# Moving the start addresses of on-chip tiles in a one-core attention block, and splitting two weight blocks one stage earlier

## The chip, the cores and the metric

The kernel runs on one core of one Trainium2 chip. The metric is the device time of one execution in microseconds. A core has TensorE (PE, matrix multiplication; its weight loads are listed apart as PEld), VectorE (DVE), ScalarE (ACT), GpSimd (POOL) and SyncE (SP, which issues most of the DMAs). Data lie in SBUF, 128 partitions of some 200 KB each; matmuls write to PSUM, in banks of 512 fp32 columns.

## The reference

One sub-layer of a hybrid encoder, in fp32, on x of 1024 tokens by 1024 channels. Cut to what matters:

```python
h = rms_norm(x, g_pre)
a_qkv, bq, bk, bv, mq, ga, gb, gm, mg = split(h @ w_in)      # 1024 x 10496 weights in all
# A: 24 heads in 3 groups, dilated sliding windows (128,1) (512,4) (2048,16), rope, merged by their lse
# B: 8 query heads on 2 key heads, qk-norm, 2-D axial rope, full attention over 1024 tokens
# M: 4 heads, cross-attention into 256 memory tokens (mem normed, @ w_mem_kv)
ya, yb, ym = (oa * silu(ga)) @ w_br_a, (ob * silu(gb)) @ w_br_b, (om * silu(gm)) @ w_br_m
merged = sum(sigmoid(mg + b_merge)[i] * y[i])                # per channel, 3 branches
return x + rms_norm(merged @ w_out, g_post)
```

## The kernel before

**Arithmetic.** An fp32 product is made of three matmuls on float32r operands: each operand is split into a high part h (an ACT copy that rounds) and a low part l = x - h (a DVE subtraction), and the products h·h, h·l and l·h are added in PSUM. `split` (lines 104 to 106) makes the two parts. The normalised x, transposed, stands in SBUF all the time as hh0 to hh7 and hl0 to hl7, each 128 channels by 1024 tokens.

**Stages, in order.** The key and value projection of B and the start of the gates and of the memory (`kv_proj`, `add_gate`, `add_kv`, lines 363 to 560); the projections of bq and mq with the memory attention woven in (`b_q`, `mq_unit`, `m_att`); B's attention with projection units of the merge gates woven in (`b_att`, `add_filler`, lines 654 to 795); the value stage (lines 799 to 1037), which makes the values of branch A; the pair stage (lines 1038 to 1359), which makes the remaining gates, A's queries and keys and the remaining merge gates; A's attention with the branch outputs woven in (lines 1360 to 1758); the output projection (lines 1759 to 1838).

**The value stage.** `steps_v` is a list of 44 steps. Steps 0 to 15 are a plain product, 8 blocks for each half of the tokens; steps 16 to 43 (FIRST = 16) are the seven products of Strassen's scheme in Winograd's form, 4 blocks each, in the order of `PRODUCTS`. A step issues 12 matmuls (line 983: four banks by three parts), then the evacuation of an earlier product (`left`), the splits and loads that are due two and five steps later, and the sums of weights. POOL makes the sums S1 to S4, ACT and DVE the splits. Steps FIRST + 24 to FIRST + 27 also split the four blocks of T2 (sums of the token operand, loaded from DRAM), which the pair stage needs; T1, T2, T3 and T4 are kept for the whole pair stage. The last evacuations follow the loop (`v_out`, `v_store`): DVE adds, ACT scales and issues the store.

**The pair stage.** `pairs` lists 26 pairs of 128-column weight units; each pair is again seven products of 12 matmuls (`prod`, line 1093, 26 x 7 x 12 = 2184 matmuls). The order of the products over the pairs is written out in `START` and `order`: (0,1), (0,2), (0,4), (0,3), (1,1), (0,5), and so on, where (n, x) is product x of pair n. TensorE works strictly in this order. After the matmuls of a product, the program queues the evacuation of the product before, and then `tasks(n, x)`: which blocks are split (`block_of`), which blocks of T3 are split (`split_block`), which weights are summed on POOL (`weight_sum`) and which are loaded. ACT, DVE, POOL and SP take their work in the order of the program in both stages (a manual schedule from line 801). Pair 0's blocks S1 and S2 lie in a `wh` and a `wl` buffer (two of each), all others in `ch` buffers. Product 4 takes S1 and T1, product 3 S2 and T2, product 5 S3 and T3. `own_blocks(n)` splits A11 and A12 of pair n.

**Where tiles lie.** Tiles are taken from two ends of SBUF, in the order of the program, each pool behind the one before, each tile rounded up to 32 bytes. At the lower end the first 1152 bytes are taken, then follow the constants: cs (1704 bytes, rounded to 1728), ones, mhalf, rb, rcol, nrcol, rsq and hbm, up to byte 7264 of each partition, which is 14 x 512 + 96. There hh0 begins; as hh, hl, wr, wh and wl are 4096 bytes each and nothing small is between, all of them begin at 96 past a multiple of 512. The pools that come and go behind them (start, qn, ba, tb, vp, sr, aa, mg) begin there too, and so do their tiles, until a small tile stands ahead: behind bnm (272 bytes) QH and QL begin at 160, and bp at 256 past a multiple of 512. The upper end is at byte 229,344, which is 447 x 512 + 480; the tiles of kvl, ml, t23, tr, rope and aqk, and with them KS, kmh, T1, T2, T3, aq and ak, begin at 480 past a multiple of 512, and wbh and wbl, behind small tiles, at 416. A streamed operand of 512 fp32 columns is 2048 bytes of a partition, a block of weights of 128 columns 512 bytes, so a slice of a tile has the remainder of its tile.

Of the kernel before, what the change touches and what calls it, by code (L numbers as in the profile page):

```python
# [8 lines left out]
F32 = mybir.dt.float32  # L9
R = mybir.dt.float32r  # L10
# [5 lines left out]
S = 1024  # L16
NT = 8
P = 128
# [32 lines left out]
def block(ctx: ExitStack, tc: tile.TileContext, x, xT, memT, cst, msk, bcst, tabA, gpost,  # L51
# [4 lines left out]
    const = ctx.enter_context(tc.tile_pool(name="const", bufs=1))  # L56
# [32 lines left out]

    cs = const.tile([P, C_END], F32, name="cs")  # L90
    nc.sync.dma_start(cs, cst)
    ident = cs[:, C_ID:C_ID + 128]
    ones = const.tile([P, 1], F32, name="ones")
    V.memset(ones, 1.0)
# [9 lines left out]
    def split(dst_h, dst_l, src):  # L104
        A.activation(dst_h, src, AF.Copy)  # L105
        V.tensor_tensor(dst_l, src, dst_h.bitcast(F32), op=OP.subtract)  # L106
# [130 lines left out]
    def pool(name, side="left"):  # L237
        p = tc.tile_pool(name=name, bufs=1, side=side, reuse_waits="tile")
        return p, p.__enter__()

    def close(p):
        p.__exit__(None, None, None)

    startp, st = pool("start")
    kvp, kvl = pool("kvl", "right")
    mlp, ml = pool("ml", "right")
# [199 lines left out]
    for k in range(8):  # L446
        if k % 2 == 0:
            load_wkv(k // 2)
        for e in range(2 if k == 0 else 1):
            t = slice(e * 512, e * 512 + 512) if k == 0 else slice(0, S)  # L450
# [29 lines left out]
    for c in range(2):  # L480
        t = st.tile([P, 4, 256], F32, name=f"mt{c}", tag=f"xk{c}")
# [327 lines left out]
    T1, T2, T3 = [], [], []  # L809
# [5 lines left out]
    def wslot(j):  # L815
        return wp.tile([P, 1024], R, name=("wh", "wl")[j])
# [40 lines left out]
    def parts_of(t):  # L857
        return t[:, lo], t[:, hi]
# [98 lines left out]
    def weight_sum(n, j, to):  # L957
        u, v, op = {1: lambda: (part(n, 2), part(n, 3), OP.add), 2: lambda: (to[1], part(n, 0), OP.subtract),
                    3: lambda: (part(n, 0), part(n, 2), OP.subtract),
                    4: lambda: (part(n, 1), to[2], OP.subtract)}[j]()  # L960
        G.tensor_tensor(to[j], u, v, op=op)
# [10 lines left out]
    for n, (i, e, k) in enumerate(steps_v):  # L972
        if k == 0:
            now = v_banks()
        for j in range(4):
            if i is None:
                t = slice(e * 512 + j * 128, e * 512 + j * 128 + 128)
                (bh, bl), w, end = (hh[k][:, t], hl[k][:, t]), v_first[k], 7
            else:
                (bh, bl), w, end = tokens_at(i, k, j), SB[i, k], 3  # L980
            wh_, wl_ = parts_of(w)
            for q, (a, b) in enumerate(((bh, wh_), (bl, wh_), (bh, wl_))):
                PE.matmul(now[j], a, b, start=k == 0 and q == 0, stop=k == end and q == 2)
        behind = left.pop(0)() if left else []
        if n + 2 < 8 and n + 2 >= 4:
            v_first.append(slots0[n - 2])
            split(*parts_of(v_first[-1]), raw1[:, n - 2])
        if 6 <= n < 20 and n % 4 == 2:
            x_scale(n // 4 - 1)
        m = n + 2 - FIRST  # L990
        if 0 <= m < 28:
            split_at(*divmod(m, 4))
        for f in behind:
            f()
        m = n + 5 - FIRST
        if 0 <= m < 28:
            blocks_at(*divmod(m, 4))
        for nm, s0 in (("S1", 7), ("S3", 11), ("S2", 17), ("S4", 21)):
            if 0 <= n - s0 < 4:
                sum_at(nm, n - s0)  # L1000
        if 6 <= n < 20 and n % 4 == 3:
            x_blocks(n // 4 - 1)
            if n < 19:
                x_load(n // 4)
        if n == 4:
            nc.sync.dma_start(rl, lbd.rearrange("h (a b) -> (h a) b", b=64))
        if n == 8:
            V.reciprocal(rl, rl)
            nc.sync.dma_start(rld.rearrange("h (a b) -> (h a) b", b=64), rl)
        if 0 <= n - FIRST - 24 < 4:  # L1010
            h, l = parts_of(T2[n - FIRST - 24])
            split(h, l, l.bitcast(F32))
        if n == FIRST + 10:
            for j in range(2):
                nc.sync.dma_start(tab[j], tabA[:, j])
        if n == FIRST + 17:
            V.tensor_tensor(tab[0], tab[0], rb, op=OP.mult)
            G.tensor_tensor(tab[1], tab[1], rb, op=OP.mult)
        if n == FIRST + 16:
            load_pair(0, 0)  # L1020
            load_pair(0, 1)
        if n == FIRST + 21:
            own_blocks(0)
        if n - FIRST in (15, 16):
            t_load("T2", T2, n - FIRST - 15)
        if n - FIRST in (19, 23):
            t_load("T3", T3, (n - FIRST - 19) // 4)
        if k == end:
            for j in range(4):
                if i is None:  # L1030
                    left.append(lambda b=now[j], T=4 * e + j: [lambda: v_store(rs(), VG[0], T, b)])
                else:
                    left.append(lambda i=i, j=j, b=now[j]: v_evac(i, j, b))
# [26 lines left out]

    def block_of(n, nm):
        src = part(n, 3) if nm == "A22" else SF[int(nm[1])]
        if n == 0 and nm in ("S1", "S2"):
            h, l = parts_of(wslot(int(nm[1]) - 1))
        else:
            t = CH.pop() if CH else sr.tile([P, 2, 512], R, name="ch", bufs=5)
            h, l = t[:, 0], t[:, 1]
        split(h, l, src)
        BL[n][nm] = h, l

# [141 lines left out]

    def tasks(n, x):
        if n < 2:
            blocks = {(0, "1"): [(0, "S1"), (0, "S2")], (0, "4"): [(0, "S3")], (1, "1"): [(1, "S1")], (0, "5"): [(0, "A22")],
                      (1, "4"): [(0, "S4")], (0, "7"): [(1, "S2")], (0, "6"): [(1, "S3")], (1, "3"): [(1, "A22")],
                      (1, "2"): [(1, "S4")], (1, "5"): [(2, "S1")], (1, "7"): [(2, "S3")], (1, "6"): [(2, "A22")]}.get((n, x), ())
        else:
            blocks = {"1": [(n, "S2")], "2" if n < last else "3": [(n, "S4")]}.get(x, [])
            if n < last:  # L1220
                blocks = {"7": [(n + 1, "S3")], "6": [(n + 1, "A22")], "5": [(n + 1, "S1")]}.get(x, blocks)
        for m, nm in blocks:
            block_of(m, nm)
        for nm, k in {(0, "1"): [("T3", 0), ("T3", 1)], (0, "2"): [("T3", 2)],
                      (0, "4"): [("T3", 3)]}.get((n, x), ()):
            split_block(nm, k)
        j = {(0, "2"): 1, (0, "4"): 2, (0, "3"): 3, (1, "4"): 4}.get((n, x))
        if j:
            weight_sum(1, j, SF)
        if n == 0:  # L1230
            if x == "5":
                for u in range(2):
                    load_pair(2, u)
        elif n < last:
            if x == "3":
                own_blocks(n + 1)
            j = {"4": 1, "3": 2, "2": 3, "5": 4}.get(x) if n > 1 else {"3": 1, "2": 2, "5": 3}.get(x)
            if j:
                weight_sum(n + 1, j, SF)
            if n == 1 and x == "5":  # L1240
                weight_sum(2, 4, SF)
            if x == ("4" if n > 1 else "3") and n + 2 <= last:
                load_pair(n + 2, 0)
                load_pair(n + 2, 1)
        if x in "325":
            for u, y in ((1, "3"), (0, "2")):
                if x == y:
                    rope_add(n - 1, u)
            for u, y in ((1, "2"), (0, "5")):
                if x == y:  # L1250
                    rope_store(n - 1, u)
        if n == last - 1 and x in "46" or n == last and x == "1":
            if x != "6":
                m_load(wp.tile([P, S], F32, name="wr", bufs=WR))
            if x != "1":
                m_load(sr.tile([P, S], F32, name="rw", bufs=2))
        if n == last and x in "4352":
            for k in (0, 1) if x in "45" else (2, 3):
                t = lo if x in "43" else hi
                split(hh[k][:, t], hl[k][:, t], MB[k][:, t])  # L1260
# [105 lines left out]
    with tc.tile_pool(name="aa", bufs=1, reuse_waits="tile") as aa:  # L1366
# [190 lines left out]
        def combine(p_):  # L1557
# [2 lines left out]
            c, wgt = {}, [None] * 3  # L1560

            def fetch():
                c["t"] = cb.tile([32, 3, 2, 64], F32, name="cpt", bufs=1)
                nc.sync.dma_start(c["t"].rearrange("c g q i -> c g (q i)"),
                                  std[p_].rearrange("g (c x) -> c g x", c=32))

# [94 lines left out]
        LR = []  # L1661

        def lse_load():
            LR.append(cb.tile([16, 512], F32, name="lse"))
            for b in range(2):
                nc.sync.dma_start(LR[0].rearrange("r (h b i) -> b r h i", h=4, b=2)[b],
                                  std[3, 0:2].rearrange("g (t b h i) -> b (g t) h i", t=8, b=2, h=4)[b])
# [295 lines left out]
```

## Time and profile before

| what | value |
| --- | --- |
| time before, median of 3 runs | 1427.84 us (1427.16 to 1429.21) |
| the profiled execution | 1427.6 us, span 1425.8 us |
| TensorE busy | 1401.5 us, 7547 instructions |
| DVE, ACT, POOL busy | 947.3, 657.9, 543.9 us |
| DMA | 204.26 MB, mean 143 GB/s |
| TensorE's mean granted clock | 0.998 |

The profile is one execution, taken by the hardware. A line such as "L1093 PE MATMUL s<-T,ch" names the code line, the engine, the operation, the tile written and the tiles read, the streamed operand first and the weights second, buffer numbers left out. Float32r is shown as f32. In the timeline, the first column is the start of an instruction in microseconds from the start of the span and the second its duration; consecutive equal instructions stand in one row with their count. Matmuls are pipelined: each takes about 0.39 us from start to end, and the next starts long before that end, so the rate is read from the starts. In brackets stands the idle time of the engine before an instruction, and what ended it. "PEclk" is the share of full clock that TensorE was granted.

### The profile page before, as it was taken

The page shows a single profiled execution, that of the slowest core. Times are in us where ns is not written, and L with a number is a line of the kernel's source. Part 1 is how long each engine was busy: PE and PEld are TensorE (multiplying, and loading weights), DVE is VectorE, ACT ScalarE, POOL GpSimd, SP SyncE. Part 2 cuts the span into 40 slices and gives each one's busy share as a digit, 9 for nine tenths or more (in the row PEclk, how much of TensorE's full clock was granted, in tenths as well). Part 3 has the DMA queues.
Part 4 walks back from the last instruction along what each step waited for, and adds up shares of the span by engine and source line. Part 5 has one row for each costly group of instructions (what it writes and reads, how often), then busy time and mean ns, then how long its engine had stood idle before and what let it go on. Part 6 is the DMA issues. An engine that isn't in the chain of part 4 may idle for free.

```text
span 1425.8 us, 21181 instructions
## 1 busy us (share of the span) xinstructions
PE 1401.5 (98%) x7547; PEld 1119.0 (78%) x7547; DVE 947.3 (66%) x1703; ACT 657.9 (46%) x1434; POOL 543.9 (38%) x437
## 2 busy tenths in 40 slices
PE   7999999999999999999999999999999999999998
PEld 7899986666657887888888888888877777777887
DVE  7765468677652477977777877655766666867543
ACT  6553355666653454443222232344447766732221
POOL 0415604677674312322554455433300012346322
PEclk9999999999999999999999999999999999999999
DMA  6342011011007674332655565756568578736223
GB/s 234 110 120 75 16 62 62 18 32 41 20 24 260 207 243 133 112 110 104 174 153 147 162 170 170 221 199 220 195 225 243 176 212 233 218 108 246 82 89 104
DMA packets 103466, 204.26 MB, mean 143 GB/s; under 512 B 19552, under 2 KB 49472, under 8 KB 103360
## 3 DMA queue, kind: packets, MB, share of 16 engines
q1 hardware_dynamic: 89584, 189.14, 42.2%
q10 hardware_dynamic: 13776, 13.77, 2.8%
q8 instruction: 59, 0.97, 0.3%
q14 instruction: 47, 0.39, 0.1%
HBM read 134.39 MB, written 55.89 MB: 133 GB/s over the span
## 4 chain that ended last, share of the span: by engine, by line
PE 51%; DMA 3%; issue 2%; DVE 2%; ACT 1%; POOL 1%; SPq 0%; ACTq 0%; DVEq 0%; POOLq 0%
PE s L1093 30%; PE d L1297 8%; PE sc L1810 5%; PE s L1441 3%; PE d L1504 3%; DMA or<-rld 2%; PE tr L1484 1%; PE tr L1475 1%; DVE rs L1140 0%; DMA od<-og 0%; DVE rs L1138 0%; POOL res L1819 0%; ACT rs L1142 0%; PE s L1696 0%; DVE ch L106 0%
## 5 line engine op out<-in xcount | busy, mean ns | idle before, releaser
L1093 PE MATMUL s<-T,ch 128*128 128x512 f32 x912 | 220.7, 395 | 0.0
L1093 PEld LDWEIGHTS s<-T,ch 128*128 128x128 f32 x912 | 171.2, 188 | 40.4
L726 POOL TENSOR_TENSOR bl<-bl,bp 128x512 f32<-128x512 f32 x96 | 123.7, 1289 | 47.9 <-ACT bp L722 42.0
L106 DVE TENSOR_TENSOR ch<-sf,ch 128x512 fp32r<-128x512 f32 x102 | 90.1, 889 | 75.5 <-ACT ch L105 75.5
L1093 PE MATMUL s<-hh,ch 128*128 128x512 f32 x408 | 129.9, 389 | 0.0
L1297 PE MATMUL d<-hh,wh 128*128 128x512 f32 x384 | 126.7, 399 | 1.2 <-DVE wl L1303 1.0
L702 DVE TENSOR_REDUCE bn<-tr 128x1 f32<-128x512 f32 x128 | 85.4, 687 | 18.8 <-PE tr L701 17.0
L722 ACT ACTIVATE bp<-s 128x512 f32<-128x512 f32 x128 | 75.9, 596 | 44.7 <-PE s L720 42.9
L1158 ACT ACTIVATE sp<-s 128x512 f32<-128x512 f32 x52 | 31.0, 596 | 125.9 <-PE s L1093 105.0
L1093 PEld LDWEIGHTS s<-hh,ch 128*128 128x128 f32 x408 | 76.6, 188 | 15.9
L1126 POOL TENSOR_TENSOR o<-o,rc 128x1024 f32<-128x1024 f32 x24 | 61.8, 2575 | 70.7 <-DMA o<-rs 41.3
L1297 PEld LDWEIGHTS d<-hh,wh 128*128 128x128 f32 x384 | 72.1, 188 | 17.2 <-DVE wl L1303 1.6
L1304 POOL TENSOR_TENSOR acc<-acc,wl 128x512 f32<-128x512 f32 x32 | 57.9, 1810 | 68.3 <-DVE wl L1303 68.3
L1093 PE MATMUL s<-hl,wh 128*128 128x512 f32 x208 | 81.3, 391 | 0.0
L1093 PE MATMUL s<-hh,wl 128*128 128x512 f32 x208 | 81.2, 390 | 0.0
L1093 PE MATMUL s<-hh,wh 128*128 128x512 f32 x208 | 81.2, 390 | 0.0
L1093 PE MATMUL s<-hl,ch 128*128 128x512 f32 x204 | 79.5, 389 | 0.0
L105 ACT ACTIVATE wh<-wr 128x1024 fp32r<-128x1024 f32 (+1 forms) x64 | 56.1, 878 | 50.5 <-DMA wr<-in_wbr 14.5
L143 PE MATMUL d<-hh,wh 128*128 128x512 f32 x192 | 76.6, 399 | 1.7 <-DVE fth L222 1.7
L1459 ACT ACTIVATE pra<-pra,sts 128x192 f32<-128x192 f32 (+2 forms) x176 | 77.3, 442 | 1.6 <-DVE sts L1451 1.6
L1297 PE MATMUL d<-hl,wh 128*128 128x512 f32 x192 | 77.8, 405 | 0.0
L147 PE MATMUL d<-hh,wl 128*128 128x512 f32 x192 | 76.5, 398 | 0.0
(398 smaller groups left out, 3578.6 us busy)
## 6 DMA issues: line engine op xcount, KB each, us to landing
wr<-in_wu SPq DMA_DIRECT2D x39, 512.0 KB, 6.7
rw<-in_wu SPq DMA_DIRECT2D x25, 512.0 KB, 4.7
o<-rs SPq DMA_DIRECT2D x96, 128.0 KB, 2.3
qkd<-o SPq DMA_DIRECT2D x24, 512.0 KB, 6.3
wl<-thd SPq DMA_DIRECT2D x24, 512.0 KB, 6.0
thd<-rs ACTq DMA_DIRECT2D x36, 256.0 KB, 2.5
aq<-qkd SPq DMA_DIRECT2D x12, 512.0 KB, 4.8
ak<-qkd SPq DMA_DIRECT2D x12, 512.0 KB, 6.3
```

What stands on the lines that cost most here:

```text
L106: V.tensor_tensor(dst_l, src, dst_h.bitcast(F32), op=OP.subtract)
L143: PE.matmul(dst, wh[:, k, :], hh[k][:, t], start=k == 0, stop=False)
L147: PE.matmul(dst, wl[:, k, :], hh[k][:, t], start=False, stop=k == 7)
L702: fp["last"] = V.tensor_reduce(st[i]["n"][:, j, c:c + 1], s, axis=AX.X, op=OP.min)
L722: A.activation(pp, s, AF.Exp, scale=-1.0)
L726: G.tensor_tensor(lsum[i % 2], lsum[i % 2], pp, op=OP.add)
L1093: PE.matmul(dst, a, b, start=opens and i == 0, stop=closes and i == 11, skip_group_check=True)
L1126: G.tensor_tensor(QO[n, u], QO[n, u], RT.pop((n, u))[0], op=OP.add)
L1297: PE.matmul(s, a, b, start=q == 0, stop=q == 11)
L1304: G.tensor_tensor(accs[f][:, h], accs[f][:, h], th[:, h], op=OP.add)
L1459: A.activation(src, src, AF.Exp, scale=-1.0, bias=sums(T, h, 0), accum_out=sums(T, h, 1))
L1810: PE.matmul(parts[h], *terms[h][j], start=j == 0, stop=j == 23)
```

## The change

The change has three parts.

A tile of 416 bytes, pad_left, is taken behind cs, and a pool with one tile of 480 bytes, pad, is taken first at the upper end. Neither is read or written.

Pair 0's S1 and S2 are summed and split in the value stage: the sums into vv0 and vv1 at steps FIRST + 24 and FIRST + 25, the splits at steps FIRST + 26 and FIRST + 27. The sums of S1 to S4 ahead of the pair stage stay. In place of those two splits, the last two blocks of T2 are split in the tasks of (0,1), and the first two blocks of T3, which were split there, move to the tasks of (0,2).

In A's attention, cpt is a tile of 2048 bytes, of which 1536 are used, and the lse tile of the last item takes the same buffer.

```diff
     nc.sync.dma_start(cs, cst)
+    const.tile([P, 104], F32, name="pad_left")
...
+    pad = ctx.enter_context(tc.tile_pool(name="pad", bufs=1, side="right"))
+    pad.tile([P, 120], F32, name="pad")
     startp, st = pool("start")
...
-        if 0 <= n - FIRST - 24 < 4:
+        if n - FIRST in (24, 25):
             h, l = parts_of(T2[n - FIRST - 24])
             split(h, l, l.bitcast(F32))
+            weight_sum(0, n - FIRST - 23, {1: vv[0], 2: vv[1]})
+        if n - FIRST in (26, 27):
+            j = n - FIRST - 25
+            BL[0][f"S{j}"] = parts_of(wslot(j - 1))
+            split(*BL[0][f"S{j}"], vv[j - 1])
...
     def block_of(n, nm):
         src = part(n, 3) if nm == "A22" else SF[int(nm[1])]
-        if n == 0 and nm in ("S1", "S2"):
-            h, l = parts_of(wslot(int(nm[1]) - 1))
-        else:
-            t = CH.pop() if CH else sr.tile([P, 2, 512], R, name="ch", bufs=5)
-            h, l = t[:, 0], t[:, 1]
+        t = CH.pop() if CH else sr.tile([P, 2, 512], R, name="ch", bufs=5)
+        h, l = t[:, 0], t[:, 1]
...
-            blocks = {(0, "1"): [(0, "S1"), (0, "S2")], (0, "4"): [(0, "S3")], (1, "1"): [(1, "S1")], (0, "5"): [(0, "A22")],
+            blocks = {(0, "4"): [(0, "S3")], (1, "1"): [(1, "S1")], (0, "5"): [(0, "A22")],
...
-        for nm, k in {(0, "1"): [("T3", 0), ("T3", 1)], (0, "2"): [("T3", 2)],
+        for nm, k in {(0, "1"): [("T2", 2), ("T2", 3)], (0, "2"): [("T3", 0), ("T3", 1), ("T3", 2)],
                       (0, "4"): [("T3", 3)]}.get((n, x), ()):
             split_block(nm, k)
...
-                c["t"] = cb.tile([32, 3, 2, 64], F32, name="cpt", bufs=1)
+                c["t"] = cb.tile([32, 512], F32, name="cpt", bufs=1)[:, 0:384].rearrange("c (g q i) -> c g q i", g=3, q=2)
...
-            LR.append(cb.tile([16, 512], F32, name="lse"))
+            LR.append(cb.tile([32, 512], F32, name="lse", tag="cpt", bufs=1)[0:16])
```

## The prediction, made before the result was known

> **What bounds the kernel now.** I read the page first, then the busy times by stage, the waits of TensorE, and the timeline of TensorE in each stage.
>
> ```profile
> span 1425.8 us, 21181 instructions
> PE 1401.5 (98%) x7547; PEld 1119.0 (78%) x7547; DVE 947.3 (66%) x1703; ACT 657.9 (46%) x1434; POOL 543.9 (38%) x437
> ```
>
> TensorE is busy for 98% of the span; no other engine is above 66%. The stages say the same (columns: stretch, its length, then PE, PEld, DVE, ACT, POOL busy, granted clock, DMA share, GB/s):
>
> ```profile
> 0.00:35.00 35.00, 26.80 (x206) 26.09 (x207) 26.95 (x38) 24.09 (x33) 2.68 (x6) 1.00 0.67 234
> 500.00:510.00 10.00, 10.00 (x46) 8.29 (x45) 8.85 (x13) 6.41 (x12) 1.05 (x1) 1.00 0.67 211
> 510.00:520.00 10.00, 10.00 (x45) 8.29 (x45) 9.45 (x13) 5.95 (x11) 2.44 (x1) 1.00 0.84 271
> 557.00:570.00 13.00, 10.28 (x38) 7.75 (x38) 7.84 (x10) 9.62 (x16) 3.28 (x2) 0.88 0.70 210
> 800.00:900.00 100.00, 100.00 (x437) 81.72 (x436) 75.57 (x86) 28.46 (x48) 54.77 (x32) 1.00 0.59 164
> ```
>
> TensorE idles only in the first 35 us, at 557 to 570, and at the end. So the time is the sum of the spacings from one matmul to the next, and the question is whether the change alters a spacing. A busy TensorE says nothing of that; the starts in the timeline do (columns: start us, duration us, engine, line, shape, count):
>
> ```profile
> 78.55 0.28 PE L536 MATMUL d<-mh,wh 128*128 128x256 f32 x1
> ...
> 80.59 0.28 PE L536 MATMUL d<-mh,wl 128*128 128x256 f32 x1
> ```
> ```profile
> 584.15 0.62 PE L1093 MATMUL s<-hh,ch 128*128 128x512 f32 x2
> ...
> 586.19 0.61 PE L1093 MATMUL s<-hh,ch 128*128 128x512 f32 x2
> ...
> 587.10 2.95 PE L1093 MATMUL s<-T,ch 128*128 128x512 f32 x12
> 589.89 0.39 PE L1093 MATMUL s<-hh,wh 128*128 128x512 f32 x1
> ```
>
> - 256 columns, mh and wh: 17 starts from 78.55 to 80.59, 120.0 ns each.
> - 512 columns, hh with ch: 9 starts from 584.15 to 586.19, 226.7 ns each.
> - 512 columns, T with the same kind of ch: 12 from 587.10 to 589.89, 232.5 ns each.
>
> The first two differ by 106.7 ns for 256 columns. So 512 columns stream in 213.3 ns, and each matmul carries a bubble of 13.3 ns besides, whatever its length. For T the bubble is 19.2 ns. T and hh have the same shape, type and weights buffer; they differ in where they lie. By the allocations, hh, hl, mh, wh, wl, sl and ch begin at 96 bytes past a multiple of 512, and T, KS and the other tiles of the upper end at 480 past one; QH and QL at 160, wbh and wbl at 416. All of these are 32 past a multiple of 64. So the bubble goes with the start address, and no full-rate matmul of this trace has an operand on a rounder one.
>
> One group comes near: the tiles bp begin at 256 past a multiple of 512. They are fp32 and stream at half rate, so the comparison is weak.
>
> ```profile
> 304.28 0.40 PE L145 MATMUL d<-hl,wh 128*128 128x512 f32 x1
> 304.61 3.65 PE L735 MATMUL ov<-bp,VS 128*64 128x512 f32 x16
> 308.19 0.50 PE L147 MATMUL d<-hh,wl 128*128 128x512 f32 x1
> ```
>
> 16 passes take 3.58 us, 16 x 213.3 is 3.41, and a change of kind alone costs 0.10 (304.28 to 304.61 is 0.33 instead of 0.23). That leaves 0.07 us, about 4 ns a pass.
>
> **The change part by part. 1, the two pads.** They add no instruction; they move every tile of the lower end behind cs up by 416 bytes and every one of the upper end down by 480. The tiles at 96 and at 480 come to 0, and these are the operands of nearly all matmuls. Tiles that lie behind small ones don't: QH, QL and the mqh family come to 64, wbh and wbl to 448, mph to 384, and bp goes from 256 to 160. What a matmul on a multiple of 512 takes is not in the trace. Its bounds: 213.3 ns below (no bubble), 226.7 above if the bubble is the instruction's own, 232.5 if such addresses are as bad as T's. I take 216, near the lower end, because the bp passes carry 4 ns or less, and because a bubble that is the same for 256 and for 512 columns and equals 32 of them (32/512 of 213.3 is 13.3) is what one more block of 128 bytes to fetch at a ragged start would give; that is a conjecture from these rows. For 256 columns I take 109.
>
> The Trainium skill's page "TensorE: Matmul & The Clock Gate", section "Wait — 56ns, not 53.3ns?", gives 215.7 ns from start to start for 512 columns on a warm clock, with about 2.5 ns as a fixed cost. The trace disagrees: its clock is 1.00 and its best steady spacing is 226.7; by the page alone the sum below would be larger by about 1.4 us.
>
> The remaining spacings, and the count of the largest group:
>
> ```profile
> 84.97 0.40 PE L145 MATMUL d<-hl,wh 128*128 128x512 f32 x1
> ...
> 86.81 0.39 PE L143 MATMUL d<-hh,wh 128*128 128x512 f32 x1
> ```
> ```profile
> 95.92 0.28 PE L303 MATMUL s<-wbh,hh 128*128 128x256 f32 x1
> ...
> 98.04 0.28 PE L303 MATMUL s<-wbh,hh 128*128 128x256 f32 x1
> ```
> ```profile
> 301.04 0.40 PE L701 MATMUL tr<-KS,QH 128*128 128x512 f32 x1
> ...
> 302.21 0.39 PE L147 MATMUL d<-hh,wl 128*128 128x512 f32 x1
> ```
> ```profile
> 1380.26 0.62 PE L1810 MATMUL sc<-hl,wh 128*128 128x512 f32 x2
> ...
> 1387.51 0.61 PE L1810 MATMUL sc<-hh,wl 128*128 128x512 f32 x2
> ```
> ```profile
> 557.40:1070.00 512.60, 503.86 (x2184) 411.00 (x2184) 1.00 0.55 170
> ```
>
> Counts other than the 2184 of line 1093 are those of the loops in the code.
> - Line 1093: 2184 at 228.8 ns (437 in 100 us): 12.8 x 2184 = 28.0 us.
> - Lines 983, 1297 and 1810: 528 + 576 + 360, all taken at line 1810's 226.7 (32 starts from 1380.26 to 1387.51): 10.7 x 1464 = 15.7.
> - Lines 143 to 147: 576 at 230 (8 from 84.97 to 86.81): 14 x 576 = 8.1.
> - Line 701 with KS: 128 at 234 (5 from 301.04 to 302.21): 18 x 128 = 2.3.
> - 256 columns on mh and in line 1810: 240 at 120: 11 x 240 = 2.6.
>
> That is 56.7 us. The operands that end at 64, 384 or 448 could gain all or nothing: 288 of 512 columns on QH, QL, blh and bll at 18 ns (5.2), 768 of 256 columns at 117.8 (18 from 95.92 to 98.04; 8.8 each, 6.8). I take half of 12.0, so 62.7 in all. With no bubble at all and every operand served it would be about 83. For bp the cost lies between nothing and a bubble of 13.3 ns on 256 passes, 3.4 us; I take nothing, since at half rate there is room for one more line.
>
> What covers this: the shorter TensorE must not run into another engine. DVE has 8.85 and 9.45 of 10 us at 500 to 520, and 5% less time for that leaves almost nothing; in the first 35 us the matmuls wait for splits and loads anyway, so line 373 gains little. For these and for chains whose slack shrinks I take off a tenth, 6 us (between 0 and 15). Part 1: 56.7, rounded 57.
>
> **2, S1 and S2 of the first pair.** Here TensorE stands still once:
>
> ```profile
> PE s L1093 <- ACT wh L105: 2.7, 1, 2.7
> ```
> ```profile
> 557.49 0.39 PE L1093 MATMUL s<-hh,wh 128*128 128x512 f32 x1
> ...
> 562.71 0.39 PE L1093 MATMUL s<-hh,wl 128*128 128x512 f32 x1
> 565.81 4.86 PE L1093 MATMUL s<-T,wh 128*128 128x512 f32 x12 [2.72 <-ACT wh L105]
> 570.51 2.96 PE L1093 MATMUL s<-T,wl 128*128 128x512 f32 x12
> 573.31 0.39 PE L1093 MATMUL s<-hh,wh 128*128 128x512 f32 x1
> ```
>
> The step from 562.71 is 3.10 us instead of 0.23, and the next 12 take 4.70 instead of 2.75 while the granted clock of the stretch is 0.88: 4.8 us lost. S1's split sits behind the last stores of the value stage in ACT's queue:
>
> ```profile
> 563.97 0.72 ACT L900 ACTIVATE vr<-vr,rcol 128x512 f32<-128x512 f32 x1 [0.50 <-ACT vr L900]
> 565.13 0.63 ACT L105 ACTIVATE wh<-sf 128x512 fp32r<-128x512 f32 x1 [0.44 <-ACT vr L900]
> 568.22 1.04 ACT L105 ACTIVATE wh<-wr 128x1024 fp32r<-128x1024 f32 x1
> ```
> ```profile
> 567.00 4.07 DVE L106 TENSOR_TENSOR T<-T 128x512 fp32r<-128x512 f32 x3
> 570.99 1.21 DVE L106 TENSOR_TENSOR wl<-wr,wh 128x1024 fp32r<-128x1024 f32 x1
> ```
>
> The change moves both splits ahead of those stores and puts T2's last two there instead; they are needed only half-way through the fourth product, about 567 (557.49 + 42 x 0.227; 557.49 is the start of the first), and are ready near 566.5, where the low halves of S1 and S2 are now. Two more POOL sums, of at most 1.7 us each, fall where POOL idles:
>
> ```profile
> 549.91 1.67 POOL L961 TENSOR_TENSOR sf<-wr 128x512 f32<-128x512 f32 x1 [33.28 <-DVE sl L106]
> ```
>
> What is late next is the fifth product: it would start at 557.49 + 48 x 0.227 = 568.4, but its weights, split at 568.22 on ACT and 570.99 on DVE, are behind the same stores. DVE's three T splits, 4.07 us now beside POOL's sums, are then shorter, since those sums can run sooner, so I put the low half near 570.5. The product gains 3 us against 573.31, not 4.8 (bounds 0, if the clock falls again, and 4.8).
>
> **3, the renamed cpt and lse tiles** add no instruction; the lse load waits for cpt's last reader, two items earlier: nothing.
>
> **Sum.** The profiled execution took 1427.6 us, 1.8 more than its span and 0.2 below the median of 1427.84. 1427.6 - 57 - 3 = 1367.6, say 1368.
>
> **The rivals.** *Only unequal remainders cost.* TensorE reads a streamed operand and the next weights together; hh with ch (96 and 96) is the quicker, T with ch (480 and 96) the slower. Then equal zeros are as good as equal 96s, and only T's 936 gain 5.8 ns, 5.4 us, with perhaps 2 in the other mixed groups: 1427.6 - 7 - 3 = 1418. For it: hh's spacing is very even. Against it: with unequal remainders wbh has 117.8 where mh with equal ones has 120.
>
> *The address is indifferent* and T is slower for another reason, such as the order of its buffers: 1427.6 - 3 = 1425. The Trainium skill's page "SBUF — State Buffer", section "Specifications (TRN2)", gives cachelines of 16 bytes; by that rule every one of these tiles starts on a line already, and no pad could matter. The rows of hh and T speak against it. If the split gains nothing either, it is no change.
>
> *Slower.* Streamed operand and weights now start at the same place of a 512-byte block, and if the two reads meet there, hh's matmuls become like T's: 3288 of them by 5.8 ns, 19 us, so 1444 after the gain of 3. It decides if the meeting costs more than 1 ns a matmul (3 us / 3288). Against it, equal remainders are not the slow ones now.
>
> **How the numbers follow.** My forecast 0.70, unequal remainders 0.14, indifferent 0.09 (of this 0.03 within 0.2%), slower 0.05, some mixture on the faster side 0.02. So faster 0.92, same 0.03, slower 0.05; 0.2%, about 3 us, is what a measurement of this kernel can tell from no change. The forecast's own range, from the unknown bubble and the cover, is 1350 to 1390; with the first rival the range is 1350 to 1419.
>
> **What would show it.** Right: line 1093 shows T and hh alike, near 216, 800 to 900 us holds some 460 matmuls, the start to start of mh is near 109, and TensorE stays at 98%. Wrong: hh stays at 226.7 (then first or second rival), or spacings fall but TensorE's idle grows at 500 to 520 (then DVE binds). Part 2 is right if the 2.7 us wait on S1 is gone and a shorter one stands before the fifth product.

## The result, and the profile after

| | before | after |
| --- | --- | --- |
| median | 1428.53 us (4 runs, 1427.16 to 1430.72) | 1420.36 us (4 runs, 1419.99 to 1421.22) |
| ratio | | 0.9942, interval 0.9927 to 0.9958 |
| the profiled execution | 1427.6 us, span 1425.8 | 1419.99 us, span 1418.2 |

The kernel is 8 us faster, not 60. The forecast of 1368 failed, and the time is 1.4 us above the upper end of the range; it is near the 1418 of the first rival. One execution, the first of the kernel called "All at 96" below, took 5013.79 us and is left out of its median and interval. From the page of the kernel after:

```profile
PE 1395.0 (98%) x7547; PEld 1118.1 (79%) x7547; DVE 947.3 (67%) x1703; ACT 657.8 (46%) x1434; POOL 547.6 (39%) x439
```

TensorE still bounds the kernel; its busy time fell by 6.5 us. One stretch of the pair stage in the kernel after (columns as before):

```profile
800.00:900.00 100.00, 100.00 (x443) 82.87 (x442) 79.53 (x89) 28.36 (x48) 56.38 (x33) 1.00 0.58 170
```

Between 800 and 900 us stand 443 matmuls instead of 437; some 460 were forecast. The starts of TensorE in the timeline of the kernel after (the diff shifts line 1093 to 1098 and 536 to 539):

```profile
77.45 0.28 PE L539 MATMUL d<-ml,wh 128*128 128x256 f32 x1
...
80.08 0.28 PE L539 MATMUL d<-mh,wl 128*128 128x256 f32 x1
```
```profile
584.12 0.39 PE L1098 MATMUL s<-hl,ch 128*128 128x512 f32 x1
...
586.38 0.39 PE L1098 MATMUL s<-hh,ch 128*128 128x512 f32 x1
586.61 2.88 PE L1098 MATMUL s<-T,ch 128*128 128x512 f32 x12
589.33 0.39 PE L1098 MATMUL s<-hh,wh 128*128 128x512 f32 x1
```

For 256 columns, 22 spacings from 77.45 to 80.08 are 119.5 ns each, as before (120.0). For hh with ch, 10 from 584.12 to 586.38 are 226 ns each, as before (226.7), though both now start at multiples of 512. Only T moved: 12 from 586.61 to 589.33 are 226.7 ns instead of 232.5. So T became equal to hh, and hh gained nothing. The prediction had named this as its sign of being wrong: hh stays at 226.7.

Where the 7.6 us between the two profiled executions lie can be read from the starts at four places. The first matmul of the pair stage starts at 557.49 before and at 558.36 after (0.87 later); the quoted start of T is at 587.10 and at 586.61 (so 1.36 gained in that stretch). The last matmul of the pair stage, before and after:

```profile
1063.68 0.39 PE L1093 MATMUL s<-hh,ch 128*128 128x512 f32 x1
```
```profile
1056.94 0.39 PE L1098 MATMUL s<-hh,ch 128*128 128x512 f32 x1
```

From T's row to there it is 476.58 us before and 470.33 after: 6.25 gained, of which the 912 matmuls on T with ch, nearly all in this stretch, make 912 x 5.8 = 5.3. From there to the end of the span another 0.86 is gained. That is -0.87 + 1.36 + 6.25 + 0.86 = 7.6.

The split of S1 and S2 shows in the stretch with the stall. TensorE and ACT in the kernel after:

```profile
558.36 0.39 PE L1098 MATMUL s<-hh,wh 128*128 128x512 f32 x1
...
563.79 2.88 PE L1098 MATMUL s<-T,wh 128*128 128x512 f32 x12
568.76 3.02 PE L1098 MATMUL s<-T,wl 128*128 128x512 f32 x12 [2.08 <-ACT sp L1163]
571.62 0.39 PE L1098 MATMUL s<-hh,wh 128*128 128x512 f32 x1
571.84 0.39 PE L1098 MATMUL s<-hl,wh 128*128 128x512 f32 x1
573.12 0.50 PE L1098 MATMUL s<-hh,wl 128*128 128x512 f32 x1 [0.89 <-DVE wl L107]
```
```profile
565.91 0.72 ACT L903 ACTIVATE vr<-vr,rcol 128x512 f32<-128x512 f32 x1 [0.50 <-ACT vr L903]
...
567.08 1.15 ACT L106 ACTIVATE T<-T 128x512 fp32r<-128x512 f32 x2 [0.44 <-ACT vr L903]
568.13 0.58 ACT L1163 ACTIVATE sp<-s 128x512 f32<-128x512 f32 x1
```

The wait on S1 is gone: the third product follows the second without a pause. Then the fourth waits 2.08 us, and the fifth 0.89. The fourth product, (0,3), adds on to the PSUM bank of the first, (0,1), and ACT must have copied that bank out before (line 1163). This copy stands in ACT's queue behind the last store scalings of the value stage and T2's two splits; it begins at 568.13. The 12 matmuls from 563.79 take 4.97 us instead of 2.72, the step from 571.84 takes 1.28 instead of 0.23, and the product between them 0.14 too much: 3.4 us lost, where it was 4.8 before. That is 1.4 us gained here, but the pair stage begins 0.87 us later, so that 0.5 is left of it in this profile. The 0.87 comes from the value stage: from its first matmul to the pair stage it is 120.0 us before (437.5 to 557.49) and 120.9 after (437.4 to 558.36). Why is not shown. The waits of TensorE hold one of 0.4 to 0.5 us for DVE in the value stage (line 986 here, at about 499 us) in the profiles of all seven kernels with the split, and none in the two without it (before, and the pads alone), though the split's own instructions come only some 45 us later.

### The profile page after: what moved, and what is told of

Its sections match the earlier page's. It is cut to its first block, busy times and chain, and to the rows that moved or that the text cites. A ratio compares the mean times of both kernels' runs of the same rounds, so it can differ in the third digit from the quotient of the medians.

```text
span 1418.2 us, 21184 instructions
## 1 busy us (share of the span) xinstructions
PE 1395.0 (98%) x7547; PEld 1118.1 (79%) x7547; DVE 947.3 (67%) x1703; ACT 657.8 (46%) x1434; POOL 547.6 (39%) x439
## 4 chain that ended last, share of the span: by engine, by line
PE 56%; DVE 2%; issue 2%; ACT 1%; POOL 0%; ACTq 0%; POOLq 0%; DVEq 0%
PE s L1098 34%; PE d L1302 9%; PE sc L1815 5%; PE s L1446 3%; PE d L1509 3%; PE tr L1489 1%; PE tr L1480 1%; POOL res L1824 0%; DVE T L107 0%; PE s L1701 0%; ACT vr L903 0%; DVE rs L1143 0%; PE d L1098 0%; DVE res L1823 0%; DVE ot L1556 0%
## 5 line engine op out<-in xcount | busy, mean ns | idle before, releaser
L1098 PE MATMUL s<-T,ch 128*128 128x512 f32 x912 | 215.1, 390 | 0.0
L106 ACT ACTIVATE wh<-wr 128x1024 fp32r<-128x1024 f32 (+1 forms) x64 | 56.1, 878 | 50.4 <-DMA wr<-in_wbr 20.9
L1302 PE MATMUL d<-hl,wh 128*128 128x512 f32 x192 | 77.8, 405 | 0.0
L146 PE MATMUL d<-hl,wh 128*128 128x512 f32 x192 | 76.7, 399 | 0.0
```

The source lines that it names most:

```text
L146: PE.matmul(dst, wh[:, k, :], hl[k][:, t], start=False, stop=False)
L1098: PE.matmul(dst, a, b, start=opens and i == 0, stop=closes and i == 11, skip_group_check=True)
L1302: PE.matmul(s, a, b, start=q == 0, stop=q == 11)
```

## The experiments

The theories were these. **Start address**, the forecast's: a matmul whose operands start on a rounder address loses its bubble. **Agreement**, the first rival's: what counts is whether the streamed operand and the weights start at the same place, whatever that place is. **Indifferent**: neither counts, and T gained for another reason.

**A bench of matmuls alone.** The kernel computes nothing of the reference. It fills tiles m (streamed) and w (weights) that start at the remainder of their letter modulo 512 bytes (a 0, b 32, c 64, d 96, e 128, f 256, g 480, h 416), and runs groups of 96 matmuls back to back, at 512, 256 and 128 columns, then in bfloat16, then with 64 weight columns instead of 128. In the loop, a and b are the two remainders in columns of 4 bytes:

```python
for i in range(96):
    u, v = a + i % 2 * 512, b + i % 8 * 128
    PE.matmul(o[0:rows, 0:n], wt[w][:, v:v + rows], mv[m][:, u:u + n], start=i == 0, stop=i == 95)
```

> A kernel of matmuls alone, with no part of the reference's computation: 28 groups of 96 matmuls, one after the other, each group with its own remainder of the streamed operand and of the weights (bytes past a multiple of 512), its own width and its own type. Theory 1 (unequal remainders cost, the bubble of 13.3 ns is the instruction's own): 512 columns of float32r take 226.7 ns from start to start for every equal pair (0 and 0, 32 and 32, 96 and 96, 480 and 480) and more, up to 233, for unequal pairs. Theory 2 (the place itself counts, a rounder one is better): 0 and 0, 64 and 64, 256 and 256 are quicker than 32 and 32, 96 and 96, 480 and 480, and 256 streamed with weights at 0 is as quick as 0 with 0. If the bubble belongs to the type, bfloat16 of 512 columns takes clearly less than 226.7; if it belongs to the load of 128 weight columns, weights of 64 columns take less.

The timeline of TensorE in the bench; the step from one row's start to the next, divided by 96, is the spacing:

```profile
75.11 21.96 PE L52 MATMUL s<-md,wd 128*128 128x512 f32 x96
96.91 21.97 PE L52 MATMUL s<-mf,wf 128*128 128x512 f32 x96
118.72 21.95 PE L52 MATMUL s<-mg,wg 128*128 128x512 f32 x96
140.50 22.55 PE L52 MATMUL s<-ma,wb 128*128 128x512 f32 x96
162.89 22.56 PE L52 MATMUL s<-ma,wc 128*128 128x512 f32 x96
185.29 22.64 PE L52 MATMUL s<-ma,wd 128*128 128x512 f32 x96
207.76 22.46 PE L52 MATMUL s<-ma,we 128*128 128x512 f32 x96
230.06 21.93 PE L52 MATMUL s<-ma,wf 128*128 128x512 f32 x96
251.83 22.55 PE L52 MATMUL s<-ma,wg 128*128 128x512 f32 x96
274.22 22.57 PE L52 MATMUL s<-mb,wa 128*128 128x512 f32 x96
296.62 22.15 PE L52 MATMUL s<-mc,wa 128*128 128x512 f32 x96
318.61 22.57 PE L52 MATMUL s<-md,wa 128*128 128x512 f32 x96
...
407.60 22.46 PE L52 MATMUL s<-md,wg 128*128 128x512 f32 x96
429.90 22.46 PE L52 MATMUL s<-mg,wd 128*128 128x512 f32 x96
452.20 11.68 PE L52 MATMUL s<-ma,wa 128*128 128x256 f32 x96
463.71 11.68 PE L52 MATMUL s<-md,wd 128*128 128x256 f32 x96
475.23 11.47 PE L52 MATMUL s<-mc,wa 128*128 128x256 f32 x96
486.53 11.47 PE L52 MATMUL s<-mh,wd 128*128 128x256 f32 x96
497.84 10.83 PE L52 MATMUL s<-ma,wa 128*128 128x128 f32 x96
```

Equal remainders take 226.9 to 227.2 ns, whether both are 96 (md, wd), 256 or 480, and the rows left out show the same for 32 and 64. The group with both at 0 is the first and takes in the start-up; its last 69 matmuls, from 15.88 to the next group's start at 31.52, take 226.7. So the absolute start counts for nothing. Remainders 0 and 32, 64, 96, 128 or 480 take 232.3 to 234.1, with one exception: streamed at 64 with weights at 0 (mc, wa) takes 229.1, while the other way round (ma, wc) takes 233.3. The pair of the kernel before, 96 and 480, takes 232.3 both ways (md, wg and mg, wd). Remainders 0 and 256 (ma, wf) take 226.8: so the two must agree modulo 256 bytes, not 512. With 256 columns the order is reversed: equal 119.9 and 120.0, unequal 117.7 and 117.8. That is the difference that the prediction held against this rival, and it is real. With 128 columns the group takes (10.83 - 0.275) / 95 = 111.1 ns, only 9 less than with 256. Weights of 64 columns don't shorten the spacing at 512 columns: (22.34 - 0.393) / 95 = 231.0 ns, with both starts at 0.

The bfloat16 groups of the same kernel, in the busy times by form (busy time of the group, mean ns of one):

```profile
L58 PE MATMUL s<-nb,yb 128*128 128x512 bf16 x96 | 20.9, 379 | 0.0
...
L58 PE MATMUL s<-nb,yb 128*128 128x256 bf16 x96 | 10.6, 272 | 0.0
```

The group's time less its last matmul, over 95 spacings: (20.9 - 0.379) / 95 = 216.0 ns, and (10.6 - 0.272) / 95 = 108.7. The second row is rounded too far for what follows; in the timeline the last 93 matmuls of that group take 10.32 us, and (10.32 - 0.272) / 92 is 109.2. If a matmul is a constant and a part that grows with the columns, the constant is 2 x 109.2 - 216.0 = 2.4 ns for bfloat16 and 2 x 120.0 - 227.1 = 12.9 for float32r with equal starts. For float32r this working has its limits: streamed at 64 with weights at 0 it gives 2 x 117.7 - 229.1 = 6.3, and at 128 columns it would give some 66 ns where 111.1 were measured. What holds without it is that float32r takes 11 ns more than bfloat16 at 512 columns, and that no start address tried brings it below 226.7.

**All at 96.** The kernel after, with the lower end where it was and the upper end moved to 96: equal remainders, but none round.

```diff
-    const.tile([P, 104], F32, name="pad_left")
...
-    pad.tile([P, 120], F32, name="pad")
+    pad.tile([P, 96], F32, name="pad")
```

> The changed kernel with one pad instead of two: nothing at the lower end, 384 bytes at the upper, so that the large tiles of both ends begin at 96 past a multiple of 512: equal, but not round. Theory 1 (equal remainders are what counts): line of the pair stage shows T at 226.7 ns like hh, and the time is that of the changed kernel, ratio to before 0.994. Theory 2 (a round start counts): T stays near 232.5, and the time is only the split's share better, ratio 0.998 to 0.999.

Measured: 1422.57 us (1420.4 to 1422.81 in 5 runs), ratio 0.9957 (0.9943 to 0.9971). The same kernel was run once more for its profile:

> The kernel of e2_equal96 once more (every large tile at remainder 96, the streamed operand and the weights alike), for an undisturbed profile of the T products. If agreement of the two starts modulo 256 bytes is what counts and the absolute start is not: the T products on ch at 226.7 ns, 443 matmuls between 800 and 900 us, the time about 1421 us (1419 to 1423). If a start at a multiple of 512 bytes is worth something by itself: more than 226.7 ns or fewer than 443, and a time some us above that of the change.

It took 1421.55 us in one run, beside 1428.42 for the kernel before. That stretch and its timeline:

```profile
800.00:900.00 100.00, 100.00 (x443) 82.77 (x442) 79.27 (x89) 28.37 (x48) 56.41 (x33) 1.00 0.59 169
```
```profile
586.97 2.88 PE L1097 MATMUL s<-T,ch 128*128 128x512 f32 x12
589.69 0.39 PE L1097 MATMUL s<-hh,wh 128*128 128x512 f32 x1
```

T takes 2.72 / 12 = 226.7 ns with both operands at 96, and 443 matmuls stand between 800 and 900 us. Of the two pads, the one at the upper end alone brings the gain; its interval overlaps that of the change, so the multiple of 512 itself brings nothing that can be seen.

**The upper end at 256, and at 128.** The kernel after with a smaller right pad; the lower end stays at 0.

```diff
-    pad.tile([P, 120], F32, name="pad")
+    pad.tile([P, 56], F32, name="pad")      # upper end at 256
...
+    pad.tile([P, 88], F32, name="pad")      # upper end at 128
```

> The changed kernel with 224 bytes at the upper end instead of 480: lower tiles at 0, upper tiles at 256 past a multiple of 512: round, but not equal. Theory 1: T is slow again, 229 to 233 ns, and 5 to 6 us of the gain are lost, ratio to before 0.998 to 0.999. Theory 2, and theory 1 with a period of 256 bytes or less: T at 226.7 and ratio 0.994.

> The changed kernel with 352 bytes at the upper end instead of 480: lower tiles at 0, upper tiles at 128 past a multiple of 512, so the two differ by 128, as in the change's forerunner they differ by 128 counted in 256 (96 and 224). Theory 1 as the chain of matmuls left it (the streamed operand and the weights must agree counted in 256): T takes 232 to 233 ns again, the pair stage has about 437 matmuls in 100 us instead of 443, 5.5 to 6.5 us of the gain are lost, ratio to before 0.998 to 0.999. Theory 2 (a rounder start is enough): T at 226.7, ratio 0.994.

At 256: 1420.84 us (1420.29 to 1424.03 in 5 runs), ratio 0.9949 (0.9937 to 0.9962); its trace has T's 12 from 586.79 to 589.51, 226.7 ns each, and 443 matmuls between 800 and 900 us. At 128: 1427.16 us (12 runs, 1425.63 to 1431.88), ratio 0.9998 (0.9988 to 1.0008). The timeline at 128:

```profile
587.33 2.96 PE L1098 MATMUL s<-T,ch 128*128 128x512 f32 x12
590.12 0.39 PE L1098 MATMUL s<-hh,wh 128*128 128x512 f32 x1
```

T is back at 2.79 / 12 = 232.5 ns, and the whole gain is gone, with every large tile at a multiple of 128 and the split of S1 and S2 still in place. Agreement modulo 256 holds in the kernel as in the bench, and "indifferent" is out: between the last two kernels only the size of one pad differs.

**The pads alone, and the split alone.** The first is the kernel before with both pads and the cpt and lse tiles of the change, the second the kernel after without the pads. Both have the third part of the change.

```diff
+    const.tile([P, 104], F32, name="pad_left")      # the pads alone: these, added to before
+    pad.tile([P, 120], F32, name="pad")
...
-    const.tile([P, 104], F32, name="pad_left")      # the split alone: these, taken from after
-    pad.tile([P, 120], F32, name="pad")
```

> The pads and the renamed small tiles without the split of S1 and S2 in the value stage. Both theories: the part of the pads alone. From the two traces it is 6.6 us of T's spacing and 0 to 0.6 of the start, so 1421 to 1422 against 1428.5, ratio 0.995 to 0.996. If the split is worth the 3 us that were forecast, it is 1424, ratio 0.997.

> The change without both pads: S1 and S2 of the first pair in the value stage alone. By the trace of the changed kernel the fourth product then waits 2.1 us for a PSUM bank, whose copy stands behind the last four stores in ACT's queue, and the fifth 0.9 for its weights, so of 4.8 us lost there about 1.4 come back: 1427 against 1428.5, ratio 0.999. The forecast had 3 us, ratio 0.998. T stays at 232.5.

Pads alone: 1421.4 us (1420.49 to 1422.53 in 5 runs), beside 1428.85 for the kernel before, ratio 0.995 (0.9937 to 0.9962). Split alone: 1427.92 us (11 runs, 1426.09 to 1432.23), ratio 1.0001 (0.9992 to 1.0011). So the pads carry all of the gain that can be measured; the split is worth at most about 1 us. TensorE with the pads alone, and with the split alone:

```profile
566.51 5.49 PE L1096 MATMUL s<-T,wh 128*128 128x512 f32 x12 [2.77 <-ACT wh L106]
571.80 3.33 PE L1096 MATMUL s<-T,wl 128*128 128x512 f32 x12
```
```profile
565.28 2.96 PE L1095 MATMUL s<-T,wh 128*128 128x512 f32 x12
570.19 3.05 PE L1095 MATMUL s<-T,wl 128*128 128x512 f32 x12 [1.95 <-ACT sp L1160]
...
573.31 0.40 PE L1095 MATMUL s<-hl,wh 128*128 128x512 f32 x1
575.41 0.50 PE L1095 MATMUL s<-hh,wl 128*128 128x512 f32 x1 [1.70 <-DVE wl L106]
```

With the pads alone the old stall is there in full, a pause of 2.77 us and then 12 matmuls in 5.29 us instead of 2.72. With the split alone there are two pauses, 1.95 before the fourth product and 1.70 before the third matmul of the fifth. Two pauses of 3.65 us in all stand in place of the one of 2.72 in the kernel before; as 12 slowed matmuls followed that one (4.70 us), the loss, counted as above, is 4.1 us instead of 4.8.

**QH and QL moved too.** The bnm tiles of the kernel after are made 512 bytes long, so that QH, QL and blh start at 0 as KS does, and bp at 96.

```diff
-    nmt = [ql_.tile([P, 68], F32, name=f"bnm{i}") for i in range(2)]
+    nmt = [ql_.tile([P, 128], F32, name=f"bnm{i}")[:, 0:68] for i in range(2)]
```

> The changed kernel with the two bnm tiles made 512 bytes long instead of 272, so that QH, QL, blh and bll begin at 0 past a multiple of 512, as KS and KB do, instead of 64; bp goes from 160 to 96. Theory 1: lines 704, 722 and 723 fall from some 233 to 226.7 in their undisturbed spacings, 384 x 6 ns = 2.3 us and a few tenths at their neighbours; ratio to before 0.992 to 0.993. If what slows them is the change from one kind of matmul to another, nothing: ratio 0.994. The bp passes (fp32, half rate) keep their 224 ns in both.

Measured: 1420.21 us (1417.99 to 1421.39), ratio 0.9943 (0.9931 to 0.9955), beside 0.9942 for the change: no difference that can be measured. The spacings didn't fall either: in B's attention, where lines 704, 722 and 723 alternate with projections, six spacings from 300.22 to 301.63 us are 235 ns each, where the kernel of the change has 234 (five from 300.65 to 301.82), and the busy times of the three lines are 50.8, 52.3 and 50.7 us beside 51.0, 52.4 and 50.7. So agreement does not by itself give 227 ns: where matmuls of different kinds alternate, something else holds the spacing. The second branch of the expectation fits, but what it is was not tested.

**A shorter chain into the pair stage.** The kernel of the run before, with T2's four splits back in the value stage, two steps earlier, beside those of S1 and S2, and with the last four value stores issued by SP instead of ACT.

```diff
-        return lambda: v_store(r, VG[1 + u], 4 * t + j, r, t > 0)
+        return lambda: v_store(r, VG[1 + u], 4 * t + j, r, t > 0 or u == 1)
...
+        if 0 <= n - FIRST - 22 < 4:
+            h, l = parts_of(T2[n - FIRST - 22])
+            split(h, l, l.bitcast(F32))
         if n - FIRST in (24, 25):
-            h, l = parts_of(T2[n - FIRST - 24])
-            split(h, l, l.bitcast(F32))
...
-        for nm, k in {(0, "1"): [("T2", 2), ("T2", 3)], (0, "2"): [("T3", 0), ("T3", 1), ("T3", 2)],
+        for nm, k in {(0, "2"): [("T3", 0), ("T3", 1), ("T3", 2)],
```

> The kernel of the bnm tiles, with T2's four splits two steps sooner in the value stage, all four there, and the last four value stores issued by SP instead of ACT. If the waits at the start of the pair stage are made by ACT's queue behind those stores, the fourth and the fifth product no longer wait, and 3 us of the 3.4 lost there come back: ratio 0.990 to 0.991. If the waits only move on (to the sixth product, or to DVE), 0 to 1 us: ratio as without it, 0.992 to 0.993.

Measured: 1420.78 us (1418.85 to 1421.13), ratio 0.9946 (0.9934 to 0.9958): no gain over the change. TensorE, and then SP and ACT, in its timeline:

```profile
570.23 0.50 PE L1099 MATMUL s<-hh,wh 128*128 128x512 f32 x1 [1.55 <-ACT wh L106]
...
571.49 0.79 PE L1099 MATMUL s<-hh,wl 128*128 128x512 f32 x1 [0.53 <-DVE wl L107]
572.08 0.63 PE L1099 MATMUL s<-hh,wh 128*128 128x512 f32 x1
```
```profile
564.57 0.54 SPq L942 DMA_DIRECT2D wr<-in_wu  x1
```
```profile
569.12 1.06 ACT L106 ACTIVATE wh<-wr 128x1024 fp32r<-128x1024 f32 x1 [2.99 <-DMA wr<-in_wu]
```

The wait on the PSUM bank is gone, and the next one stands: the high half of the fifth product's weights is 1.55 us late, its low half 0.53. From 572.08 the matmuls start 0.42 us apart instead of 0.23, for five spacings: the granted clock fell after the pauses (0.83 in the stretch from 570 to 580 us), as it did before the change (0.88 from 557 to 570).

The edit made the new wait itself, at least in part. SP issues the load of the fifth product's weights at 564.57, behind the four stores that it took over from ACT; in the kernel of the change it does so at 560.79. ACT then stands idle for 2.99 us until that load has landed, and only then splits these weights. So the run shows that the wait on the bank can be cleared, and not what a shorter chain into the pair stage is worth.

## Why the prediction was wrong, point by point

**The bound** was right: TensorE sets the time, and only its spacings count. DVE did not become the bound, but as TensorE gained 7 us and not 57, the 6 us taken off for lost cover were never put to the test; they had no part in the error, as they were set against unserved operands that gained nothing either.

**The step that failed** is "So the bubble goes with the start address", and with it the 216 ns. Two differences were put down to one cause. The 5.8 ns between T and hh do come from where the tiles lie, but from T and ch being unequal, not from 480 being a worse place than 96. The 13.3 ns that all float32r matmuls carry were in the trace as a constant, and nothing in it tied them to an address: hh with ch shows 226 ns at 0 as at 96. In the bench no start brings 512 columns of float32r below 226.7, and bfloat16 takes 216.0. Nor is the bubble the same "whatever its length": two lengths fit any line, and the third that the bench has, 128 columns, lies far off it (111.1 ns, not some 66). Of the sum of 56.7 us only T's part was there, 912 x 5.8 = 5.3 us and a little on the few other matmuls with T; the 51 us for everything else were nothing.

**The witness for 216**, the bp passes with 4 ns or less, was of another kind. The group in the busy times by form, before and after:

```profile
L735 PE MATMUL ov<-bp,VS 128*64 128x512 f32 x256 | 58.5, 599 | 0.0
```
```profile
L738 PE MATMUL ov<-bp,VS 128*64 128x512 f32 x256 | 58.5, 599 | 0.0
```

bp moved from 256 to 160 and its 256 passes take the same 58.5 us. Its small rest was not that of a round address; the prediction called the comparison weak and then took its value from it.

**The first rival** had the mechanism, and its 7 us for unequal remainders were right: the pads alone gain 7.4 us by the medians (5.4 to 9.0 by the interval of the ratio). Of these, its 5.4 us for T are what the traces show; its 2 us in other mixed groups can't be told from noise, and QH and QL, moved to equal starts, gained nothing. Two things in it were off. The pair need only agree modulo 256 bytes, and its 1418 also counted the 3 us of the split. The objection to it, that unequal operands with 256 columns were quicker, was a true row with a wrong conclusion: the sign differs between 256 and 512 columns, as the bench shows.

**The Trainium skill's** 215.7 ns for 512 columns (page "TensorE: Matmul & The Clock Gate", section "Wait — 56ns, not 53.3ns?") agrees with the bench's 216.0 for bfloat16 and not with the 226.7 to 227.2 of float32r. The forecast was nearer to this figure than to any row of its own trace. The 16-byte lines of the Trainium skill's page "SBUF — State Buffer", section "Specifications (TRN2)", fit one half of the result: 32, 96, 256 and 480 are as good as each other when both operands have them. They don't cover the other half, that two operands, each on a line, cost 5 to 7 ns (2 in one pair) when they differ modulo 256.

**"Slower"** held that two reads at the same place might meet. They do not: equal places are the quicker ones at 512 columns. **The third part**, cpt and lse, gained nothing, as forecast: with the split and without the pads the ratio is 1.0001.

**Part 2**, the split, was forecast at 3 us. The 4.8 us lost before were right, the wait on S1 went as forecast, and a shorter wait did stand before the fifth product. What was missed is the fourth product's bank: it is the first product's, and the copy that must come before is ACT's work, behind the stores and the two splits that the change puts there. The change was costed by the operands of the products and not by the buffer they write. Measured, it is 1.4 us at the start of the pair stage, 0.5 with what the value stage loses, and nothing that the times can show (1.0001, interval 0.9992 to 1.0011). Clearing this wait as well left one before the fifth product, in part by the edit that cleared it.

What stays open: why float32r takes 11 ns more at 512 columns, by which mechanism the streamed operand and the weights disturb each other, and whether it is a matmul's own weights or those loaded for the next that must agree, as within each group all weights have one remainder. bfloat16 operands have half the bytes, so type and size are not told apart here.

## What to carry to other kernels

When two groups of matmuls of the same shape differ in their spacing, compare each pair of operands before blaming one place: here a pad of some hundred bytes that made two ends of SBUF agree modulo 256 bytes was worth 0.5%, and moving everything to round addresses added nothing. A cost that is the same in every row of a trace, while the supposed cause doesn't vary either, is no evidence for that cause; a bench of a few groups settles it in one run. When an operand is made ready sooner, follow the output buffer of the next products too, and the queue of the engine that empties it. When DMA issues move from one queue to another, look at what will stand behind them there.

## What the runs showed of the hardware

- In a run of like matmuls, one of float32r and 512 columns takes 227 ns from start to start when the byte addresses of streamed operand and weights agree modulo 256, and 232 to 234 when they don't; streamed at 64 with weights at 0 takes 229.1. At 256 columns it is 120.0 when they agree and 117.8 when they don't.
- Where matmuls of different kinds alternate in B's attention, the spacing stays at some 235 ns though both operands start at multiples of 512.
- A bfloat16 matmul takes 216.0 ns at 512 columns and 109.2 at 256, so float32r with equal starts costs 11 ns more for the same columns.
